# Expert weights in longer runs, one more slot for them, and embedding inputs on another DMA queue, in a hybrid transformer layer on one core

## The chip, the cores and the metric

The kernel runs on one core of a Trainium2 chip. The metric is the time of one execution on the device in microseconds (us), as the median of several runs. A core has five engines with instruction streams of their own: TensorE (PE; its weight loads, PEld, overlap its matmuls), VectorE (DVE), ScalarE (ACT), GpSimd (POOL) and SyncE (SP). SP computes nothing here; it issues DMAs. POOL issues DMAs too, the indirect ones (gather and scatter by row numbers) among them. All DMAs of the core are carried out by its 16 DMA engines.

## The reference

One layer over 1024 tokens of width 1024, in float32:

```
x = x + concat(attention(x), mlstm(x)) @ w_o          # norms, projections, two kinds of heads
h = rmsnorm(x) * g;  pick 1 of 4 groups, then 2 of its 8 experts for each token, weights w1, w2
y = (silu(h @ w_gate_e) * (h @ w_up_e)) @ w_down_e    # 32 experts, gate and up 1024 x 256, down 256 x 1024
x = x + w1 * y[first expert] + w2 * y[second expert]
x = x + (p @ w_ple) * sigmoid((rmsnorm(x) * g2) @ w_ple_gate)   # p: 1024 x 256, an embedding for each token
out = rmsnorm(x) * g3
```

## The kernel before

Matrix products keep float32 precision by splitting: each operand becomes `hi` (rounded to the short mantissa that TensorE reads as fp32r) and `lo` (the rest), and three matmuls stand for one (`mm3`, lines 127 to 129). A split (`split`, lines 132 and 133) is a copy to `hi` on ScalarE and a subtraction to `lo` on VectorE. Weights therefore arrive raw, are split, and only then multiplied.

The execution has four stages. Until about 430 us: projections, attention and mLSTM (the first stage). Until about 548: the output projection and the router, tile by tile of 128 tokens. Then the row numbers of each expert's tokens are worked out, and the expert stage runs from about 562 to 911. The last stage sums the experts' rows and does the embedding gate and the final norm.

*The expert stage* (`experts`). Each of the 32 experts takes a block of up to 128 tokens (rows beyond that go through a loop, `overflow`, which ran for no block here). For each expert: POOL gathers its tokens from `h2d` into `xg` (`moe_gather`, line 1149; two buffers, one gather is issued two experts ahead), TensorE transposes them (`xgp`, line 1159) and both halves are split to `xh`, `xl`; gate and up are one product of 512 columns (`gups`); `silu` and the product give `eh`, which is transposed (`ehp`, line 1179), split to `eht` and multiplied with the down weights (`eyps`); the rows go through `ey` by a scatter on POOL to `ybd` (line 1189).

*The weights of the experts.* An expert has three raw tiles of 128 partitions x 2048 floats, 1 MB each: two for gate and up (`rgu`, loaded by `load_gu`, each by one DMA for gate and one for up), one for down (`rdn`, `load_dn`). All go through the SP queue, but for the two `rgu` of expert 3, which POOL issues. `R()` hands out the slots for raw tiles from a ring (`rring`): four slots in the output stage (pool R1, tags R0 to R3), nine from the expert stage on (R4 to R8 in pool R2 are added). `W()` hands out nine slots (`NW`) for split weights in the same way; a raw tile fills two, an expert six. Loads are issued three experts ahead (`moe_load(e + 3)`); a load waits until the splits have freed its slot.

*The embedding.* Six of the eight tiles of `p @ w_ple` are computed between experts, behind experts 14, 16, 18, 20, 22 and 24 (`PLE_AT`): `ple_in(i)` (line 1285) loads 128 x 256 floats into `pin`, `ple_tile(i)` (line 1302) transposes them (`pps`, line 1305), splits them and multiplies. The load for a tile is written in the code one expert ahead of its use (`if e + 1 in PLE_AT[1:]`), the first one with `ple_load` at expert 5, and the last two in `final_load`. `pin` shares its four buffers with `eh` (tag "eh"), and its load goes through the SP queue. The results are kept in `ples`: each second tile takes one raw slot out of the ring for good (`retire`), three in all.

*What sets the order.* The code is written as a sequence with tiles and buffers; a scheduler orders each engine's instructions at build time, with `issue_after` and priorities as its limits. On the chip each engine, SP and POOL too, carries out its list strictly in that order: an issue that has to wait for a free buffer holds everything behind it on its queue.

Of the kernel before, what the change touches and what calls it, by code (L numbers as in the profile page):

```python
# [20 lines left out]
P = 128  # L21
T = 1024
D = 1024
# [4 lines left out]
DE = 256  # L28
# [31 lines left out]
class Kernel:  # L60
# [1047 lines left out]
        return w[e] if isinstance(e, int) else w[bass.ds(e, 1)].rearrange("o k f -> (o k) f")  # L1108

    def load_gu(self, e, b, q=None):  # L1110
        raw = self.R("rgu")
        v = raw.rearrange("p (k u f) -> p k u f", k=4, u=2)
        for u, n in enumerate(("w_gate_e", "w_up_e")):
            w = self.weight(n, e).rearrange("(p k) f -> p k f", k=KT)
            (q or self.nc.sync).dma_start(v[:, :, u, :], w[:, 4 * b:4 * b + 4, :])
        return raw

    def load_dn(self, e):
# [22 lines left out]
        return out  # L1141

    def split_gu(self, raws):
        return [(h[:, o:o + 512], l[:, o:o + 512]) for h, l in self.split_w(raws) for o in (0, 512)]

    def moe_gather(self, gcol):
        xg = self.xgs[self.ngather % len(self.xgs)]
# [135 lines left out]
        self.ple_in(0)  # L1283

    def ple_in(self, i):
        self.pin[i] = self.t("B", "pin", [P, DE], bufs=4, tag="eh")
        self.nc.sync.dma_start(self.pin[i], self.a["p"][0, 0, i * P:(i + 1) * P, :])

    def ple_half(self, k):
        raw = self.t("PL", "rple", [P, D])  # L1290
# [131 lines left out]
    def run(self):  # L1422
        self.raws, self.nr, self.nw = {}, 0, 0
        self.mixers()
        self.open("R1", "left")
        self.open("W1", "left")
        self.rring = [("R1", f"R{i}") for i in range(4)]
        self.wring = [("W1", f"W{i}") for i in range(6)]
        self.open("RT", "right")
        self.open("A3", "right")  # L1430
        self.open("psB", None, PSUM)
        self.out_weights()
        self.router_setup()
        gb = self.bcast("A3", self.a["norm_ffn_g"][0], "gb_ffn")
        end = None
        for i in range(NT):
            end = self.out_tile(i, gb, end)
            if i == 1:
                self.raws[0] = self.moe_load(0)
            if i == 4:  # L1440
                list(self.route_tiles(0, 4))
                self.first = self.split_gu(self.raws[0][:2]), self.split_w(self.raws[0][2:])
            if i == 5:
                self.raws[1] = self.moe_load(1)
        rt = self.route_tiles(4, 7)
        next(rt)
        end()
        list(rt)
        gu2 = self.load_gu(2, 0)
        self.close("A3")  # L1450
        list(self.route_tiles(7, 8))
        self.route_static()
        self.open("R2", "left")
        self.open("B", "left")
        self.rring, self.nr = [("R2", f"R{i}") for i in range(4, 9)] + [self.rring[(self.nr + i) % 4] for i in range(4)], 0
        more = [("B", f"W{i}") for i in range(6, 9)]
        self.wring += more[:NW - 6]
        self.rring[5:5] = more[NW - 6:]
        self.raws[2] = gu2, self.load_gu(2, 1), self.load_dn(2)
        self.moe_setup()  # L1460
        with self.tc.issue_after(self.stored.ins):
            gu3 = self.load_gu(3, 0, self.nc.gpsimd)
        with self.tc.issue_after(self.routed.ins):
            self.route_rest()
        self.experts(gu3)
        self.n_over = self.nc.values_load(self.nov[0:1, 0:1], min_val=0, max_val=15)
        self.final_load()
        self.overflow()
        self.final()
        self.finish()  # L1470
# [30 lines left out]
```

## Time and profile before

| | |
|---|---|
| time, median of 3 runs | 1031.0 us (1030.45 to 1031.9) |
| the profiled execution | 1031.45 us; span from the first to the last instruction 1029.7, so 1.75 around it |
| mean granted TensorE clock | 0.966 |
| busy: TensorE, VectorE, ScalarE, GpSimd | 953.9 us (93%), 805.8 (78%), 666.7 (65%), 165.7 (16%) |
| DMA queue of SP (q1) | 146.00 MB in 111502 packets, 42.4% of the 16 engines' span |
| software DMA queue (q0, issued by POOL) | 38.33 MB in 15776 packets, 10.4% |
| packets under 2 KB | 105070 of 127360 |

The busy share of an engine is a mean over all four stages, each of which has another limit. So the rows further down are of stretches of the execution: a window gives the busy time of each engine in it (with the count of its instructions), the granted clock of TensorE (1.00 is its upper level of 2.4 GHz, 0.50 the lower of 1.2) and the share and rate of the DMA engines. A timeline row is one instruction: its start, its duration, engine, line, and in brackets the idle time in front of it with what ended that. "SPq" marks time in which SP's queue was held on an instruction.

### The profile page before, as it was taken

Reading aid. Unit: us, or ns where it says so; the run is one execution under the profiler, and the core shown is the slowest. Engines: PE = TensorE matmul, PEld = TensorE weight load, DVE = VectorE, ACT = ScalarE, POOL = GpSimd, SP = SyncE. Lnnn points to the kernel's source line nnn. Section 1 sums busy time; section 2 is a strip of 40 time slices with the busy share of each in tenths; the row PEclk is TensorE's granted clock in tenths of the full one; section 3 lists DMA queues with packets and bytes.
Section 4 is the critical chain, followed back from the end, with each engine's and each line's share of the span. In section 5 each row is a group of like instructions: output and inputs, shape, how many; then the busy total and the mean of one; then the engine's idle time right before and its main releaser. Section 6 shows DMA issues by size and latency. Waiting matters only on the chain. (4 is left out here: it accounts for less than half of the span.)

```text
span 1029.7 us, 16040 instructions
## 1 busy us (share of the span) xinstructions
PE 953.9 (93%) x5583; PEld 819.2 (80%) x5583; DVE 805.8 (78%) x1877; ACT 666.7 (65%) x1182; POOL 165.7 (16%) x213
## 2 busy tenths in 40 slices
PE   4999999998999999899995989999699999979996
PEld 4999999996788888688884867888588888858875
DVE  7759788367888989774747899998678889858885
ACT  5554766254788889763333877998578788755432
POOL 4000000101222322101013121222112112210000
PEclk9999999999999999899996998999899999989999
DMA  7230111310000001698348898999999999774541
GB/s 220 101 101 25 42 62 59 102 37 11 17 11 14 13 12 23 229 295 288 123 159 272 261 359 283 354 351 343 338 301 315 341 304 356 243 254 173 184 164 61
DMA packets 127360, 185.36 MB, mean 180 GB/s; under 512 B 19487, under 2 KB 105070, under 8 KB 123182
## 3 DMA queue, kind: packets, MB, share of 16 engines
q1 hardware_dynamic: 111502, 146.00, 42.4%
q0 software_dynamic: 15776, 38.33, 10.4%
q8 instruction: 44, 0.72, 0.3%
q14 instruction: 38, 0.31, 0.1%
HBM read 167.48 MB, written 33.59 MB: 195 GB/s over the span
## 5 line engine op out<-in xcount | busy, mean ns | idle before, releaser
L133 DVE TENSOR_TENSOR w<-rgu,w 128x1024 fp32r<-128x1024 f32 x128 | 155.1, 1227 | 32.8 <-ACT w L132 29.6
L132 ACT ACTIVATE w<-rgu 128x1024 fp32r<-128x1024 f32 x128 | 133.3, 1065 | 6.1 <-PE gups L129 3.3
L127 PE MATMUL inp<-hh,win 128*128 128x256 f32 x384 | 111.7, 291 | 0.0
L129 PE MATMUL inp<-hh,win 128*128 128x256 f32 x384 | 111.1, 290 | 0.5 <-DVE win L256 0.5
L128 PE MATMUL inp<-hl,win 128*128 128x256 f32 x384 | 111.4, 291 | 0.1
L127 PE MATMUL gups<-w,xh 128*128 128x512 f32 x256 | 103.8, 405 | 0.0
L128 PE MATMUL gups<-w,xh 128*128 128x512 f32 x256 | 102.0, 398 | 0.0
L129 PE MATMUL gups<-w,xl 128*128 128x512 f32 x256 | 101.2, 395 | 0.0
L133 DVE TENSOR_TENSOR w<-rdn,w 128x1024 fp32r<-128x1024 f32 x64 | 77.2, 1219 | 2.7 <-ACT w L132 1.9
L129 PEld LDWEIGHTS inp<-hh,win 128*128 128x128 f32 x384 | 74.6, 195 | 0.7 <-DVE win L256 0.7
L128 PEld LDWEIGHTS inp<-hl,win 128*128 128x128 f32 x384 | 74.6, 194 | 0.5 <-DVE hl L133 0.4
L127 PEld LDWEIGHTS inp<-hh,win 128*128 128x128 f32 x384 | 74.5, 194 | 0.3 <-ACT z L331 0.2
L132 ACT ACTIVATE w<-rdn 128x1024 fp32r<-128x1024 f32 x64 | 66.0, 1067 | 4.1 <-PE gups L129 3.7
L1149 POOL DMA_INDIRECT xg<-h2d,gidx x32 | 37.1, 1159 | 179.2 <-PE xgp L1159 145.8
L1188 ACT ACTIVATE ey<-eyps 128x512 f32<-128x512 f32 x64 | 38.2, 596 | 40.4 <-PE eyps L129 30.8
L705 PE MATMUL po<-pt,V 128*128 128x256 f32 x320 | 61.2, 307 | 0.9 <-ACT pt L132 0.5
L133 DVE TENSOR_TENSOR pt<-ptp,pt 128x512 fp32r<-128x512 f32 (+2 forms) x112 | 54.3, 491 | 7.3 <-ACT pt L132 5.7
L132 ACT ACTIVATE pt<-ptp 128x512 fp32r<-128x512 f32 (+2 forms) x112 | 48.1, 443 | 14.7 <-PE ptp L693 7.4
L127 PE MATMUL eyps<-w,eht 128*128 128x512 f32 x128 | 54.5, 426 | 2.4 <-ACT eht L132 2.3
L129 PEld LDWEIGHTS gups<-w,xl 128*128 128x128 f32 x256 | 48.3, 189 | 9.5
L128 PEld LDWEIGHTS gups<-w,xh 128*128 128x128 f32 x256 | 48.6, 190 | 9.1
L127 PEld LDWEIGHTS gups<-w,xh 128*128 128x128 f32 x256 | 48.7, 190 | 9.0 <-ACT xh L132 0.2
(392 smaller groups left out, 2633.2 us busy)
## 6 DMA issues: line engine op xcount, KB each, us to landing
rdn<-in_w_down_e_dram SPq DMA_DIRECT2D x32, 1024.0 KB, 8.9
rgu<-in_w_gate_e_dram SPq DMA_DIRECT2D x62, 512.0 KB, 11.5
rgu<-in_w_up_e_dram SPq DMA_DIRECT2D x62, 512.0 KB, 10.0
wraw<-in_w_in_dram SPq DMA_DIRECT2D x11, 512.0 KB, 5.4
x<-in_x_dram SPq DMA_DIRECT2D x8, 512.0 KB, 4.6
abw<-mlrows SPq DMA_DIRECT2D x8, 512.0 KB, 3.7
mixf<-mixd SPq DMA_DIRECT2D x8, 512.0 KB, 5.7
xres<-in_x_dram SPq DMA_DIRECT2D x8, 512.0 KB
```

Of the source, the lines that this page charges most:

```text
L127: nc.tensor.matmul(out, w_hi, m_hi, start=start, stop=False)
L128: nc.tensor.matmul(out, w_hi, m_lo, start=False, stop=False)
L129: nc.tensor.matmul(out, w_lo, m_hi, start=False, stop=stop)
L132: a = self.nc.scalar.activation(hi, src, AF.Copy)
L133: v = self.nc.vector.tensor_sub(lo, src, hi)
L705: nc.tensor.matmul(po, self.V[kt][:, h, :], pts[t - 1][:, w, u, :], start=(kt + w == 0), stop=(kt == 2 * j + 1 and w == 1))
L1149: self.gathered = self.nc.gpsimd.indirect_dma_start(out=xg, out_offset=None, in_=self.h2d, in_offset=bass.IndirectOffsetOnAxis(ap=gcol, ax ...
L1188: nc.scalar.activation(y[:, s], py[c], AF.Copy)
```

## The change

Four edits.

1. A raw tile of gate and up held, in each partition, four runs of 512 floats, gate and up side by side, so that the DMA wrote and read 256 floats (1 KB) at a time. Now its first half holds gate and its second half up, 1024 floats in one run (4 KB). `split_gu` therefore no longer takes a flat run of 1024 for a split: it reads and writes through a view of 2 x 2 x 256 (half, row, column), and the split tiles are laid out as before.
2. The loads of `pin` are issued by POOL instead of SP, and `pin` has three buffers of its own instead of a share of the four of `eh`.
3. The scratch for DMA descriptors is set to 2048 bytes (16384 where nothing is said, an eighth), and a tenth raw slot (tag R9, pool R1) is in the ring, from the output stage on.
4. With the fifth slot of the output stage, the second half of expert 2's gate and up is loaded in front of `self.close("A3")`.

```
     def load_gu(self, e, b, q=None):
+
         raw = self.R("rgu")
-        v = raw.rearrange("p (k u f) -> p k u f", k=4, u=2)
         for u, n in enumerate(("w_gate_e", "w_up_e")):
             w = self.weight(n, e).rearrange("(p k) f -> p k f", k=KT)
-            (q or self.nc.sync).dma_start(v[:, :, u, :], w[:, 4 * b:4 * b + 4, :])
+            (q or self.nc.sync).dma_start(raw[:, u * D:(u + 1) * D].rearrange("p (k f) -> p k f", k=4),
+                                          w[:, 4 * b:4 * b + 4, :])
         return raw
...
     def split_gu(self, raws):
-        return [(h[:, o:o + 512], l[:, o:o + 512]) for h, l in self.split_w(raws) for o in (0, 512)]
+
+        out = []
+        side = lambda t: t.rearrange("p (k u f) -> p u k f", k=2, u=2)
+        for raw in raws:
+            v = raw.rearrange("p (u k f) -> p u k f", u=2, k=4)
+            for j in range(2):
+                hi, lo = self.W("w")
+                self.last_split = self.split(side(hi), side(lo), v[:, :, 2 * j:2 * j + 2, :])
+                out += [(hi[:, o:o + 512], lo[:, o:o + 512]) for o in (0, 512)]
+        return out
...
     def ple_in(self, i):
-        self.pin[i] = self.t("B", "pin", [P, DE], bufs=4, tag="eh")
-        self.nc.sync.dma_start(self.pin[i], self.a["p"][0, 0, i * P:(i + 1) * P, :])
+        self.pin[i] = self.t("B", "pin", [P, DE], bufs=3)
+        self.nc.gpsimd.dma_start(self.pin[i], self.a["p"][0, 0, i * P:(i + 1) * P, :])
...
-        self.rring = [("R1", f"R{i}") for i in range(4)]
+        self.rring = [("R1", f"R{i}") for i in (0, 1, 2, 3, 9)]
...
-        gu2 = self.load_gu(2, 0)
+        gu2 = self.load_gu(2, 0), self.load_gu(2, 1)
         self.close("A3")
...
-        self.rring, self.nr = [("R2", f"R{i}") for i in range(4, 9)] + [self.rring[(self.nr + i) % 4] for i in range(4)], 0
+        self.rring, self.nr = [("R2", f"R{i}") for i in range(4, 9)] + [self.rring[(self.nr + i) % 5] for i in range(5)], 0
...
-        self.raws[2] = gu2, self.load_gu(2, 1), self.load_dn(2)
+        self.raws[2] = *gu2, self.load_dn(2)
...
-    nc = bacc.Bacc("TRN2", target_bir_lowering=False, num_devices=1)
+    nc = bacc.Bacc("TRN2", target_bir_lowering=False, num_devices=1, dynamic_dma_scratch_size=2048)
```

On TensorE, VectorE and ScalarE the order of the instructions stays as it was but for a few neighbours that change places. On the two queues it moves. SP's list around the load of the second embedding input, before: `rgu` and `rdn` are raw expert weights, `pin` the embedding input.

```order
L1120 DMA rdn<-in_w_down_e_dram 128x2048
L1115 DMA rgu<-in_w_gate_e_dram 128x4x256
L1115 DMA rgu<-in_w_up_e_dram 128x4x256
L1287 DMA pin<-in_p_dram 128x256
L1115 DMA rgu<-in_w_gate_e_dram 128x4x256
L1115 DMA rgu<-in_w_up_e_dram 128x4x256
L1120 DMA rdn<-in_w_down_e_dram 128x2048
```

And in the changed kernel, at the same place:

```order
L1121 DMA rdn<-in_w_down_e_dram 128x2048
L1115 DMA rgu<-in_w_gate_e_dram 128x1024
L1115 DMA rgu<-in_w_up_e_dram 128x1024
L1121 DMA rdn<-in_w_down_e_dram 128x2048 x2
L1115 DMA rgu<-in_w_gate_e_dram 128x1024
L1115 DMA rgu<-in_w_up_e_dram 128x1024
```

The load of `pin` is gone from SP, and the weights stand without it; the pieces of gate and up are 1024 floats a partition instead of four times 256.

POOL's list from the first gathers of the expert stage to its first scatter, before; `xg` are the gathered tokens (two buffers, with a number behind the name), `ybd` the experts' results.

```order
L1149 DMA xg_6431<-h2d,gidx 128x1024
L1149 DMA xg_6432<-h2d,gidx 128x1024
L1115 DMA rgu<-in_w_gate_e_dram 128x4x256
L1115 DMA rgu<-in_w_up_e_dram 128x4x256
L1149 DMA xg_6431<-h2d,gidx 128x1024
L1149 DMA xg_6432<-h2d,gidx 128x1024
L1149 DMA xg_6431<-h2d,gidx 128x1024
L1149 DMA xg_6432<-h2d,gidx 128x1024
L1189 DMA ybd<-ey,sidx 2048x1024
```

The same stretch of POOL in the changed kernel:

```order
L1159 DMA xg_6431<-h2d,gidx 128x1024
L1159 DMA xg_6432<-h2d,gidx 128x1024
L1115 DMA rgu<-in_w_gate_e_dram 128x1024
L1115 DMA rgu<-in_w_up_e_dram 128x1024
L1159 DMA xg_6431<-h2d,gidx 128x1024
L1159 DMA xg_6432<-h2d,gidx 128x1024
L1297 DMA pin<-in_p_dram 128x256 x3
L1159 DMA xg_6431<-h2d,gidx 128x1024
L1159 DMA xg_6432<-h2d,gidx 128x1024
L1199 DMA ybd<-ey,sidx 2048x1024
```

Three loads of `pin`, as many as it has buffers, stand behind the fourth gather; the other five come later, each with a scatter to `ybd` ahead of it and one behind it.

## Rows read from the trace of the kernel before

**Rows 1.** Windows: us, busy (xcount) PE, PEld, DVE, ACT, POOL, clock, DMA share, GB/s.
```profile
640.00:680.00 40.00, 40.00 (x196) 33.12 (x195) 39.08 (x44) 36.77 (x54) 10.51 (x10) 1.00 1.00 353
720.00:760.00 40.00, 31.99 (x141) 25.85 (x140) 25.96 (x30) 25.06 (x38) 6.54 (x6) 0.87 0.92 317
800.00:840.00 40.00, 40.00 (x193) 32.73 (x192) 34.49 (x39) 33.40 (x50) 7.78 (x7) 1.00 0.94 315
```

**Rows 2.** Waits of TensorE, 400 to 1030 us: total us, count, mean us.
```profile
PE pps L1305 <- DMA pin<-in_p_dram: 7.5, 1, 7.5
PE xgp L1159 <- DMA xg<-h2d,gidx: 6.2, 1, 6.2
```

**Rows 3.** Timeline of TensorE: start and duration in us, idle time before in brackets.
```profile
711.81 0.39 PE L1179 MATMUL ehp<-ident,eh 128*128 128x128 f32 x2
712.04 0.40 PE L1305 MATMUL pps<-ident,pin 128*128 128x128 f32 x2
...
734.63 0.39 PE L1179 MATMUL ehp<-ident,eh 128*128 128x128 f32 x2
742.51 0.67 PE L1305 MATMUL pps<-ident,pin 128*128 128x128 f32 x2 [7.49 <-DMA pin<-in_p_dram]
742.84 0.77 PE L127 MATMUL gups<-w,xh 128*128 128x512 f32 x1
...
748.56 0.39 PE L127 MATMUL eyps<-w,eht 128*128 128x512 f32 x1
748.79 0.39 PE L128 MATMUL eyps<-w,eht 128*128 128x512 f32 x1
```

**Rows 4.** Timeline of the SP queue around the second embedding input.
```profile
722.04 2.18 SPq L1115 DMA_DIRECT2D rgu<-in_w_up_e_dram  x1
...
729.90 4.23 SPq L1287 DMA_DIRECT2D pin<-in_p_dram  x1
```

**Rows 5.** Timeline of POOL, 540 to 1030 us.
```profile
552.10 0.54 POOL L914 DMA_DIRECT2D x2d<-xres  x1
...
573.57 0.98 POOL L1149 DMA_INDIRECT xg<-h2d,gidx  x1 [4.86 <-PE xgp L1159]
...
719.02 1.36 POOL L1189 DMA_INDIRECT ybd<-ey,sidx  x1 [9.49 <-ACT ey L1188]
...
750.84 1.36 POOL L1189 DMA_INDIRECT ybd<-ey,sidx  x1 [18.71 <-ACT ey L1188]
...
772.89 1.35 POOL L1189 DMA_INDIRECT ybd<-ey,sidx  x1 [8.59 <-ACT ey L1188]
```

**Rows 6.** DMA issues, 640 to 720 us: count, KB each, median us to landing.
```profile
rgu<-in_w_gate_e_dram SPq DMA_DIRECT2D x14, 512.0 KB, 15.4
rgu<-in_w_up_e_dram SPq DMA_DIRECT2D x14, 512.0 KB, 12.1
...
xg<-h2d,gidx POOLq DMA_INDIRECT x8, 8.3
```

**Rows 7.** Window right behind the pause of TensorE.
```profile
742.00:748.00 6.00, 5.49 (x14) 4.44 (x15) 1.65 (x2) 1.33 (x2) 0.00 (x0) 0.50 0.96 356
```

**Rows 8.** Timeline of ScalarE: two splits of weights.
```profile
715.76 1.06 ACT L132 ACTIVATE w<-rgu 128x1024 fp32r<-128x1024 f32 x1 [2.81 <-DMA rgu<-in_w_up_e_dram]
...
743.50 1.05 ACT L132 ACTIVATE w<-rgu 128x1024 fp32r<-128x1024 f32 x1
```

**Rows 9.** Windows in which one kind of weight load ran alone.
```profile
542.00:544.00 2.00, 2.00 (x13) 1.65 (x11) 1.83 (x13) 0.60 (x1) 0.00 (x0) 1.00 0.88 207
546.00:550.00 4.00, 1.97 (x17) 1.59 (x16) 3.79 (x24) 1.38 (x4) 0.00 (x0) 1.00 1.01 417
```

**Rows 10.** Groups of VectorE by shape: busy us, mean ns, idle before, releaser.
```profile
L133 DVE TENSOR_TENSOR w<-rgu,w 128x1024 fp32r<-128x1024 f32 x128 | 155.1, 1227 | 32.8 <-ACT w L132 29.6 <-DMA rdn<-in_w_down_e_dram 0.5
...
L133 DVE TENSOR_TENSOR wq<-rawq,wq 128x768 fp32r<-128x768 f32 x2 | 1.9, 958 | 0.0
```

**Rows 11.** First line of the page.
```profile
span 1029.7 us, 16040 instructions
```

## The prediction

> **What bounds the kernel now.** I read the stretches first, then the waits of TensorE, then the pauses one by one on the engines and queues around them. In the expert stage the stretch 640 to 680 us has TensorE busy for all of its 40 us, VectorE for 39.08, and the DMA engines at share 1.00 with 353 GB/s; 800 to 840 again has TensorE at 40.00, with VectorE at 34.49 and DMA at 0.94 [rows 1]. So TensorE sets the pace there, and whatever another engine or a queue saves is worth nothing unless TensorE stands still for it. Between them lies one stretch that differs: 720 to 760, TensorE busy 31.99 of 40 and granted clock 0.87 [rows 1].
>
> The waits of TensorE after 400 us name the reason: the longest is the transpose `pps` of an embedding tile, 7.5 us, once, for the DMA of `pin` [rows 2]. The reader is to see in its timeline that the transposes `ehp` start at 734.63 and `pps` only at 742.51, while for the embedding tile before, `ehp` at 711.81 is followed by `pps` at 712.04 [rows 3]. The SP queue tells why the input is late: the load of that `pin` stands behind a run of expert weights, SP reaches it at 729.90, and is held on it for 4.23 us [rows 4]. ScalarE and VectorE stand still with TensorE, because their next instruction in order is the split of `pps`.
>
> **The change, part by part.**
>
> *Embedding inputs on the GpSimd queue, in three buffers of their own.* The order of the change has three `pin` loads on POOL right behind the fourth gather and ahead of the fifth. In the trace of before the fifth starts at 573.57 after 4.86 us of idle time [rows 5]. An issue on POOL costs about 0.54 us (the nearest row, a plain store of 128 rows [rows 5]), three 1.6 us, all inside that idle time. So the input of the second embedding tile is issued near 570 and used near 735; even the slowest median landing in the row list, 15.4 us [rows 6], leaves it 150 us early. The wait goes.
>
> What it is worth: `pps` follows `ehp` by 712.04 - 711.81 = 0.23 us when its input is there [rows 3], so it moves from 742.51 to 734.63 + 0.23 = 734.86: 7.65 us. Behind the pause the clock is at 0.50, its lower level of 1.2 GHz, from 742 to 748 [rows 7]: fourteen matmuls of 512 columns start from 742.84 up to 748.56, in 5.72 us, where the next two starts are 0.23 us apart [rows 3], so 14 x 0.23 = 3.22 would do: 2.50 us. Without the pause TensorE has been running for over 100 us before, as in 640 to 680 where the clock was 1.00. Together 10.15 us. A check by another view: the scatter of the expert in front of an embedding tile starts at 719.02, 750.84 and 772.89 [rows 5]; a pair of experts with one embedding tile takes 772.89 - 750.84 = 22.05 when undisturbed and 31.82 here: 9.77 us. I take 10.0.
>
> What is late next: the weight split on ScalarE that follows `pps`. It started at 743.50 [rows 8] and now could at 743.50 - 7.65 = 735.85. The second half of its tile was issued at 722.04 [rows 4]; with the median 12.1 us to landing of that queue [rows 6] it is there at 734.1, in time. Later loads are asked for at 315 GB/s (800 to 840), under the 353 that the engines gave at share 1.00 [rows 1], so the lateness does not grow. Value zero; upper end in the first rival.
>
> The five later loads add a wait on POOL: a buffer is free when the transposes of the tile three before are done. Behind the fourth load on POOL stand a scatter and two gathers. The first tile's `pps` is at 712.04 [rows 3], that scatter at 719.02 [rows 5]: 7 us to spare. For the fifth load it is 734.86 against 750.84 less 10. Nothing.
>
> The Trainium skill speaks against this part (DMA: Bandwidth & Descriptors, Issuing engines are not separate DMA queues): DMAs of all queues run on the same 16 engines and interleave, so another issuing queue saves issue time only. By that rule the queue alone is worth little; here it is the early place on it that counts. What the rule alone would leave is the second rival.
>
> *4 KB runs for gate and up.* A pure stretch of the old pattern (gate and up of one tile in 1 KB pieces, 542 to 544) moved 207 GB/s at share 0.88; one of the down weights in 8 KB pieces (546 to 550) 417 GB/s at share 1.01 [rows 9]. So a piece four times as long is moved faster, by something between nothing and a factor 417 x 0.88 / (207 x 1.01) = 1.76 in engine time. The end does not see it: TensorE is at 40.00 of 40 in the saturated stretch as well [rows 1]. What it buys is cover: ScalarE's wait of 2.81 us for a weight at 715.76 [rows 8] should go, and the loads after 735 arrive sooner. If that cover were missing, see the first rival. Value zero, between 0 and 2.8 us saved.
>
> The Trainium skill has a rule by which this part does nothing (DMA: Bandwidth & Descriptors, Specifications: full rate from 512 B on, so 1 KB already has it). The two stretches above disagree, and the measurement decides; by either the sum is the same.
>
> *The splits read two halves of a tile in a walk of 2 x 2 x 256.* VectorE and ScalarE lose their flat access of 1024. No row has three levels; the nearest has two: 768 elements of `rawq` in eight pieces took 958 ns against 1227 for 1024 flat ones [rows 10]. At the same cost for each element, a split without its fixed part would be 1227 x 0.75 = 920, so strided access costs at most 38 ns, and less if there is a fixed part. Value zero, between -0.02 and 0.04 us for a split; the price if it is more is the last rival.
>
> *Tenth slot, descriptor scratch cut to an eighth.* Before the expert stage one more half tile is loaded early, and in it the loads run one slot ahead; no wait of TensorE there is for weights [rows 2], so this is worth zero now. A short ring has no row. It costs nothing at the least. At the most, a gather may have to stand until the one DMA before it has landed, 8.3 us by the landing of gathers [rows 6]; on the path that is only the first, for which TensorE waits 6.2 us already [rows 2]; in turn, weights that come earlier or faster beside it could shorten that wait, by all of the 6.2 at most. I take zero for both: by the code POOL's issues carry few pieces, each a row of 2 to 4 KB, and the largest store (512 B pieces) is in the first stage, with POOL far ahead.
>
> *The sum.* The profiled execution took 1031.45 us (span 1029.7 [rows 11] and 1.75 around it); less 10.0 it is 1021.45. The median of the runs shown is 1031.0, 0.45 below; the forecast for the median is 1021.2.
>
> **The rivals.**
>
> 1. *Weights take the place of the input.* For it: DMA at 1.00 and a wait for a weight at 715.76 [rows 1, 8]. If longer pieces gain nothing and the load of 722.04 takes the longer 15.4 us [rows 6], it lands at 737.4, 1.6 us after 735.85; if TensorE then stops, the slow clock comes back for 2.5 us. 1021.2 + 4.1 = 1025.3. Against it: by the code nine slots hold split weights, where an expert takes six, so the splits run ahead of TensorE; and the loads before 735 were faster. 8%.
>
> 2. *The input comes at the old time.* If POOL in fact reaches the load only next to its use, at about 729.90 as SP did, the same 16 engines serve it as they serve a gather: 8.3 us [rows 6], 738.2. The pause is then 738.2 - 734.86 = 3.3 us, the slow clock stays; 4.3 of the 10 us are gained: 1026.7. Against it: the order. 5%.
>
> 3. *The change does not take away what holds `pps`.* The profile infers the releaser and gives no landing for this load. Against it: 8.4 us from the end of its issue (734.13) to 742.51 fit a landing in that queue. No difference: 1031. 4%.
>
> 4. *Slower: the split walks cost VectorE.* Place: 640 to 680 and what is like it, about 625 to 735. VectorE has 0.92 us free in these 40, with 44 instructions, at ten for an expert (six weight splits, four others) 4.4 experts: 9.1 us and 0.21 us free for each, twelve experts in 110 us [rows 1]. Four splits for each expert change; at p us more each, the stage grows by 12 x (4p - 0.21). It decides from p = 0.26 us, where the 10 us are eaten; at 0.3 it is 11.9, 1033.1. After 735 VectorE has 5.5 us free in 40 (800 to 840 [rows 1]), enough. Against it: the 38 ns above. 5%.
>
> **How the numbers follow.** Forecast 78%, rivals 8, 5, 4 and 5%. Within 0.2% (what a measurement can tell from no change, 2.1 us) lies the third alone: 4%. Slower 5%, faster 91%. The forecast's own range is 1017 to 1023.5: the two ways to reach the sum differ by 0.4 us, a saved 2.8 us and part of the first gather's wait go down, walks and ring go up. With the first and the better part of the second rival the range is 1017 to 1026.5.
>
> **What would show it.** Right: no wait of `pps` for `pin` near 735, and TensorE busy with clock 1.00 from about 625 to 900; the three `pin` issues on POOL near 570; splits of gate and up at 1.21 to 1.27 us on VectorE; fewer packets under 2 KB and less DMA share at the same pace; gathers issued right after their transposes. Wrong: a wait of ScalarE for `rgu` near 736 that TensorE shares, gaps before gathers on POOL that end with a DMA, or VectorE's splits above 1.4 us.

## The result and the profile after

The changed kernel takes 1022.35 us (1020.31 to 1023.98, 4 runs), against 1031.05 for the kernel before (4 runs): ratio 0.9916, 95% interval [0.9901, 0.9931], 8.7 us less. A second measurement beside other kernels gave 0.9913 [0.9885, 0.9942], 1024.04 us. The forecast was 1021.2. The profiled execution is the quickest of its four, 1020.31 us with a span of 1018.5.

Windows of the changed kernel (us, busy with counts of TensorE, weight loads, VectorE, ScalarE, GpSimd; then clock, DMA share, GB/s); the first, second and last answer to [rows 1], the third to [rows 7].

```profile
640.00:680.00 40.00, 40.00 (x196) 33.07 (x195) 38.84 (x45) 36.75 (x54) 11.10 (x10) 1.00 0.98 361
720.00:760.00 40.00, 40.00 (x191) 32.73 (x190) 33.57 (x39) 32.53 (x48) 9.51 (x9) 1.00 0.97 354
...
742.00:748.00 6.00, 6.00 (x31) 4.83 (x30) 5.65 (x8) 5.07 (x7) 0.61 (x1) 1.00 1.01 379
...
800.00:840.00 40.00, 40.00 (x194) 32.73 (x194) 32.79 (x40) 32.83 (x51) 9.26 (x8) 1.00 0.93 329
```

The reader is to see that 720 to 760 is now like its neighbours: TensorE 40.00 of 40 instead of 31.99, clock 1.00 instead of 0.87, and between 742 and 748 31 matmuls instead of 14. The timeline of TensorE at the second embedding tile, which answers to [rows 3]:

```profile
733.22 0.39 PE L1189 MATMUL ehp<-ident,eh 128*128 128x128 f32 x2
733.44 0.40 PE L1315 MATMUL pps<-ident,pin 128*128 128x128 f32 x2
```

`pps` follows `ehp` by 0.22 us, without a wait. The whole pause with its slow clock is read from the next transpose `ehp`, first before and then after:

```profile
757.28 0.39 PE L1179 MATMUL ehp<-ident,eh 128*128 128x128 f32 x2
```
```profile
745.76 0.39 PE L1189 MATMUL ehp<-ident,eh 128*128 128x128 f32 x2
```

From `ehp` to `ehp` it was 757.28 - 734.63 = 22.65 us and is 745.76 - 733.22 = 12.54: 10.11 us less. TensorE's waits after 400 us (total, count, longest) no longer have the first line of [rows 2]:

```profile
PE xgp L1169 <- DMA xg<-h2d,gidx: 6.8, 2, 5.9
PE cnt L970 <- DVE M L967: 5.7, 1, 5.7
```

POOL's timeline shows the three early loads (it answers to the gather at 573.57 of [rows 5]), and SP's that an issue of weights takes 0.33 us where it took 2.18 [rows 4] (the issues of gate and up between 640 and 745 us take 0.33 to 0.44 us, where they took 0.37 to 5.96):

```profile
566.70 1.00 POOL L1159 DMA_INDIRECT xg<-h2d,gidx  x1 [1.73 <-PE xgp L1169]
567.69 1.72 POOL L1297 DMA_DIRECT2D pin<-in_p_dram  x3
572.61 1.05 POOL L1159 DMA_INDIRECT xg<-h2d,gidx  x1 [3.21 <-PE xgp L1169]
```
```profile
720.59 0.33 SPq L1115 DMA_DIRECT2D rgu<-in_w_gate_e_dram  x1
722.41 0.33 SPq L1115 DMA_DIRECT2D rgu<-in_w_up_e_dram  x1
```

The splits on VectorE cost what they did, 1227 ns in the 2 x 2 x 256 view against 1227 flat [rows 10]; the packets fell by almost four in ten, from 127360 to 78976, at the same bytes:

```profile
L133 DVE TENSOR_TENSOR w<-rgu,w 128x1024 fp32r<-128x1024 f32 x128 | 155.0, 1227 | 29.0 <-ACT w L132 24.6 <-DMA rgu<-in_w_up_e_dram 0.7 <-DMA rgu<-in_w_gate_e_dram 0.7
...
DMA packets 78976, 185.36 MB, mean 182 GB/s; under 512 B 19487, under 2 KB 40558, under 8 KB 74798
```

So far everything stands as forecast. What the forecast had not seen came out when the parts were taken one by one.

### The profile page after: what moved, and what is told of

Same layout as the page of the kernel before. It is cut to its first block, busy times and chain, and to the rows that moved or that the text cites. A ratio compares the mean times of both kernels' runs of the same rounds, so it can differ in the third digit from the quotient of the medians.

```text
span 1018.5 us, 16023 instructions
## 1 busy us (share of the span) xinstructions
PE 946.1 (93%) x5583; PEld 812.3 (80%) x5583; DVE 805.9 (79%) x1877; ACT 666.9 (65%) x1182; POOL 174.0 (17%) x221
## 2 busy tenths in 40 slices
DMA packets 78976, 185.36 MB, mean 182 GB/s; under 512 B 19487, under 2 KB 40558, under 8 KB 74798
## 5 line engine op out<-in xcount | busy, mean ns | idle before, releaser
L133 DVE TENSOR_TENSOR w<-rgu,w 128x1024 fp32r<-128x1024 f32 x128 | 155.0, 1227 | 29.0 <-ACT w L132 24.6
L1159 POOL DMA_INDIRECT xg<-h2d,gidx x32 | 39.8, 1244 | 178.1 <-PE xgp L1169 135.3
L128 PEld LDWEIGHTS gups<-w,xh 128*128 128x128 f32 x256 | 48.3, 189 | 9.2
L127 PE MATMUL wops<-wo,mixh 128*128 128x512 f32 x128 | 52.5, 412 | 3.4 <-ACT wo L132 3.4
```

The source lines that it names most:

```text
L127: nc.tensor.matmul(out, w_hi, m_hi, start=start, stop=False)
L128: nc.tensor.matmul(out, w_hi, m_lo, start=False, stop=False)
L133: v = self.nc.vector.tensor_sub(lo, src, hi)
L1159: self.gathered = self.nc.gpsimd.indirect_dma_start(out=xg, out_offset=None, in_=self.h2d, in_offset=bass.IndirectOffsetOnAxis(ap=gcol, ax ...
```

## The experiments

Ratios are to the kernel before, run beside on the same chip; "loss" and "gain" are against it.

**One part of the embedding loads, or all of it.** Three kernels change only the loads of `pin`: queue and buffers, buffers only, queue only. The first two need 3 KB of room a partition (three buffers of 256 floats), which the short scratch gives.

```
pin_pool_own     pin: bufs=3, nc.gpsimd.dma_start;  dynamic_dma_scratch_size=2048
pin_sp_own       pin: bufs=3, nc.sync.dma_start;    dynamic_dma_scratch_size=2048
pin_pool_shared  pin: bufs=4, tag="eh", nc.gpsimd.dma_start
```

> The kernel before with the embedding inputs alone moved: issued by POOL, three buffers of their own (short descriptor scratch, without which the buffers find no room; nine slots, 1 KB runs). Theory P (the early place of the load is all): three loads near 568 us on POOL, no wait of pps for pin, TensorE busy 40 of 40 us from 640 to 880, 1021 to 1023 us, as the whole change. Rival R (the longer runs carry part of it: at 1 KB the weights are late as soon as the pause no longer lets them catch up): a wait for rgu behind 735, 1024 to 1028 us.

> The same, but the loads stay on SP; with three buffers of their own the first three stand early in SP's list, the others some experts ahead of their use. Theory P: the queue plays no part, 1021 to 1023 us, no wait for pin. Rival Q (a small load on SP stands behind weights wherever it is put, and only POOL's queue is quick): a later input is late or the loads hold up weights, 1026 to 1031 us.

> The kernel before with the loads of pin on POOL and nothing else: they share the four buffers of eh, so the second one stands late, between two gathers. Theory P with POOL free of a backlog: the load is issued by about 720 and lands 8 us later, before 735; no pause, but the gather behind it waits with it for the buffer: 1021 to 1024 us. The second rival of the prediction (at a late place the queue gives only half): pause of about 3 us, 1025 to 1028 us. If the buffer is what is late (a product eh three experts back must be transposed first), the pause stays: 1030 us.

Measured: 1.0037 [1.0022, 1.0052], 1.0022 [1.0013, 1.0032] and 0.9984 [0.9968, 1.0000]. Theory P missed: the pause at 735 is gone in all three (in the third a wait for `pin` of 2.8 us is left, at 905), yet two are slower than before, and the third gains about 2 us, with an interval that reaches 1. The first of TensorE's waits in `pin_pool_own` tells half of it:

```profile
PE wops L127 <- ACT mixh L132: 9.0, 1, 9.0
PE xgp L1159 <- DMA xg<-h2d,gidx: 6.1, 1, 6.1
```

A wait of 9.0 us that the kernel before does not have, in the output stage at about 440 us, where no embedding is touched. `pin_sp_own` has the same line. `pin_pool_shared`, with the full scratch, does not have it. In that kernel POOL reaches the second load only at 724.57, some 13 us ahead of its use at 737.45, and it is in time:

```profile
723.30 1.27 POOL L1149 DMA_INDIRECT xg<-h2d,gidx  x1 [0.30 <-PE gups L129]
724.57 0.62 POOL L1287 DMA_DIRECT2D pin<-in_p_dram  x1
732.41 1.04 POOL L1149 DMA_INDIRECT xg<-h2d,gidx  x1 [7.22 <-PE xgp L1159]
```

So 12 us from the end of its issue to its use were enough; it was issued 5.3 us before SP reached it in the kernel before [rows 4], since no weights stood ahead of it on POOL. So either is enough against the pause at 735: another queue at a late place (here 5.3 us earlier than SP was, and used 2.6 us later than before), or an early place on the same queue.

**The longer runs alone.**

```
load_gu, split_gu as in the change; all else as before
```

> The kernel before with the 4 KB runs alone (gate and up in two halves, splits in the strided view). Theory P: worth nothing by itself, the load of pin stands at its old place on SP and the pause stays: 1029 to 1032 us. Rival H (in the changed kernel SP's issues of weights take 0.33 us in the stretch where they took 0.4 to 4.8 before: it is the 1 KB pieces that hold SP, and with them gone SP reaches the load of pin in time): wait for pin under 2 us, 1021 to 1024 us. The splits on VectorE 1.20 to 1.27 us in both.

Measured: 0.9997 [0.9981, 1.0013]. The rival is refuted, and in an instructive way (SP's queue, then TensorE):

```profile
730.25 0.38 SPq L1297 DMA_DIRECT2D pin<-in_p_dram  x1
...
737.70 0.39 PE L1189 MATMUL ehp<-ident,eh 128*128 128x128 f32 x2
745.21 0.67 PE L1315 MATMUL pps<-ident,pin 128*128 128x128 f32 x2 [7.12 <-DMA pin<-in_p_dram]
```

SP is no longer held on the load: 0.38 us instead of 4.23 [rows 4]. But the input comes 745.21 - 730.63 = 14.6 us after the issue, where it took 8.4 before. Where these went can be counted, since the 128 rows of `pin` (1 KB) are now the only packets between 512 B and 2 KB. DMA packets of this kernel from 733 to 735, 735 to 737, 741 to 743 and 743 to 745.5 us:

```profile
DMA packets 254, 0.78 MB, mean 389 GB/s; under 512 B 27, under 2 KB 91, under 8 KB 243
DMA packets 217, 0.53 MB, mean 264 GB/s; under 512 B 78, under 2 KB 110, under 8 KB 203
...
DMA packets 172, 0.70 MB, mean 352 GB/s; under 512 B 26, under 2 KB 34, under 8 KB 140
DMA packets 248, 0.91 MB, mean 362 GB/s; under 512 B 28, under 2 KB 44, under 8 KB 235
```

"Under 2 KB" less "under 512 B" is 64, 32, 8 and 16: three quarters of the load are through by 737, eight rows follow up to 741, and the last 24 come after that. I read the lateness as time in line behind the weights issued ahead of it, on a part of the engines, and SP's being held as the share of it that shows in SP's timeline when the pieces are short. That is not shown: the packets were not told apart by engine.

**Where the 9 us in the output stage come from.** The scratch alone, and the loads of `pin` with just as much room as they need:

```
scratch      dynamic_dma_scratch_size=2048
pin_own_13k  pin: bufs=3, nc.gpsimd.dma_start;  dynamic_dma_scratch_size=13312
```

> The kernel before with the short descriptor scratch alone. Theory S (the room that it leaves free moves SP's list in the output stage, and TensorE waits some 9 us for mixh there): 1036 to 1041 us, with the pause for pin as before. Rival (the short ring itself holds POOL's gathers or stores): gaps in front of gathers that end with a DMA, and a loss spread over the expert stage. Prediction: the scratch is worth nothing, 1030 to 1032.

> As the first of these runs (embedding inputs on POOL with three buffers of their own, nothing else), but with a descriptor scratch of 13312 instead of 2048: just the room the buffers need, so that SP's list in the output stage stays that of the kernel before. Theory S (the first run lost 9 us to a wait for mixh in the output stage, which came with the room that the short scratch left free, not with the loads): that wait is gone. Theory W (without the pause the 1 KB weights are late): TensorE lacks some 4 us of 80 between 720 and 800, 1024 to 1027 us. Theory P (the early load is all): 1020.5 to 1022.5. If 1031 or more: neither, the loads on POOL themselves cost the time.

Measured: 1.0071 [1.0046, 1.0096] (7.3 us lost, as theory S has it) and 0.9965 [0.9948, 0.9982] (3.6 us gained, 1027.35 us, the wait for `mixh` gone; nearest to theory W). ScalarE in `scratch`, and in the kernel before:

```profile
433.05 7.67 ACT L132 ACTIVATE wo<-rawo 128x1024 fp32r<-128x1024 f32 x8
440.62 1.04 ACT L132 ACTIVATE mixh<-mixf 128x1024 fp32r<-128x1024 f32 x1
```
```profile
431.54 1.04 ACT L132 ACTIVATE mixh<-mixf 128x1024 fp32r<-128x1024 f32 x1
432.49 3.89 ACT L132 ACTIVATE wo<-rawo 128x1024 fp32r<-128x1024 f32 x4
```

With 14 KB free in each partition (16384 less 2048 bytes) the scheduler puts the four loads of the raw output weights (`rawo`) seven rows earlier in SP's list, in front of the router's weights. SP reaches them some 208 us earlier (`scratch`, then the kernel before):

```profile
216.29 31.28 SPq L818 DMA_DIRECT2D rawo<-in_w_o_dram  x4
```
```profile
424.43 7.22 SPq L818 DMA_DIRECT2D rawo<-in_w_o_dram  x4
```

All eight of their splits then stand in front of the split of the first tokens, `mixh`, on ScalarE. TensorE's first matmul of this stage needs `mixh`; its wait is the 9.0 us above, 7.67 of them for these splits. That free room is the cause is read from the runs side by side: the three kernels that leave 11 or 14 KB free have the wait, and none of the others, which leave 6 KB or less (the tenth slot takes 8). POOL's gathers in `scratch` show no wait on a DMA: the short ring itself costs nothing that can be seen. In the change the tenth slot takes up most of the room, and `mixh` is split at 431.49, ahead of `wo`, as before.

**What eats the rest of the 10 us.** In `pin_own_13k` SP's list in the output stage is the old one and the pause is gone, yet 3.6 us are gained and not 10. ScalarE's timeline between 736 and 800:

```profile
742.12 1.06 ACT L132 ACTIVATE w<-rgu 128x1024 fp32r<-128x1024 f32 x1 [1.99 <-DMA rgu<-in_w_up_e_dram]
...
754.43 2.01 ACT L132 ACTIVATE w<-rgu 128x1024 fp32r<-128x1024 f32 x2 [0.84 <-DMA rgu<-in_w_up_e_dram]
...
767.76 1.06 ACT L132 ACTIVATE w<-rgu 128x1024 fp32r<-128x1024 f32 x1 [3.13 <-DMA rgu<-in_w_up_e_dram]
```

And TensorE's windows there:

```profile
720.00:760.00 40.00, 37.92 (x179) 30.28 (x178) 32.02 (x37) 31.94 (x49) 8.80 (x9) 1.00 0.98 335
760.00:800.00 40.00, 38.19 (x174) 30.25 (x173) 29.81 (x37) 28.55 (x44) 9.32 (x7) 0.96 0.98 338
```

The weights are late, as the first rival of the prediction had it. From 600 to 912 us ScalarE waits 9.0 us for `rgu` in five places, where the kernel before waits 2.8 in one. Between the transposes `ehp` at 746.40 and 784.20 lie 37.8 us; in the changed kernel the same stretch takes 777.39 - 745.76 = 31.6, as it does in the kernel before behind its pause:

```profile
746.40 0.39 PE L1179 MATMUL ehp<-ident,eh 128*128 128x128 f32 x2
...
784.20 0.39 PE L1179 MATMUL ehp<-ident,eh 128*128 128x128 f32 x2
```
```profile
777.39 0.39 PE L1189 MATMUL ehp<-ident,eh 128*128 128x128 f32 x2
```

The 6.2 us between are what the late weights cost, and 10.1 - 6.2 = 3.9 fits the 3.6 gained. In the kernel before no split behind the pause waits for `rgu`, so the pause had been giving the DMA engines 10 us to catch up. The same weights were late in `pin_pool_shared`: 9.4 us of ScalarE's waits between 700 and 800.

**Which part covers it.** The longer runs or the slot added to the moved loads, one without the other:

```
pin_own_4k_13k  as pin_own_13k, with load_gu and split_gu of the change (nine slots)
pin_slot        the change with load_gu and split_gu of before (ten slots, 1 KB)
```

> The same with the 4 KB runs of gate and up, scratch 13312, nine slots. Theory W: TensorE 40 of 40 us in 720 to 800, and with it the whole gain of the change, 1020 to 1023 us. Rival T (it is the tenth slot that lets the weights run ahead): 1024 to 1027 us as without the runs. Theory P: 1021 to 1023, the same as without them.

> The changed kernel with the old 1 KB runs (embedding inputs on POOL, tenth slot, short scratch). With nine slots and 1 KB runs ScalarE waited 9.0 us for rgu between 636 and 800. Theory U (both cover late weights; each alone leaves some): ScalarE's wait for rgu 2 to 6 us there, 1023 to 1026 us. Theory T (the slot alone is enough, the runs are worth nothing): wait under 1 us, 1021 to 1023. Theory V (the runs decide, the slot only takes up room): 1026 to 1029.

Measured: 0.9976 [0.9961, 0.9992] and 0.9980 [0.9959, 1.0000]. Neither alone gains more than the moved loads by themselves (0.9965), and the two together gain 5 us more. Longer runs with nine slots shorten ScalarE's wait for `rgu` between 636 and 800 from 9.0 to 3.0 us, but a wait for the raw embedding weights appears, and TensorE follows it at 641 with a wait of 2.9 (from the sixth transpose `ehp` to the seventh it takes 14.1 us there, 10.3 in `runs_4k` and 9.6 in the kernel before):

```profile
ACT w L132 <- DMA rgu<-in_w_up_e_dram: 3.0, 2, 2.1
ACT wp L132 <- DMA rple<-in_w_ple_dram: 2.9, 1, 2.9
```

Ten slots with 1 KB leave the stretch from 746 to 778 whole (747.92 to 779.53, 31.6 us) and are late further on, the largest time before the split at 789.67:

```profile
789.67 1.06 ACT L132 ACTIVATE w<-rgu 128x1024 fp32r<-128x1024 f32 x1 [3.85 <-DMA rgu<-in_w_up_e_dram]
```

There ScalarE's wait for `rgu` is 12.1 us from 600 to 912, against 1.1 in the changed kernel. The late weights are not gone but elsewhere: from `ehp` to `ehp`, `pin_slot` is 1.6 us longer than the changed kernel just before 735, 3.4 between 780 and 805 and 2.7 between 868 and 890, together more than the 7.1 by which `pin_own_13k` is longer up to 784. Theory U holds in its direction (both are needed), not in its size: 2 to 6 us of wait were expected between 636 and 800, and it was 7.8. The time of `pin_slot`, 1028.58, is the one that theory V gives, but by V the longer runs with nine slots should have gained, and they did not. Why one slot more only moves the lateness at 1 KB stays open, and so does how the slot and the longer runs together cover it.

**The change without its largest part, and the slot alone.**

```
no_pin  the change with pin as before (SP, tag "eh")
slot10  before, with the tenth slot, the short scratch, the earlier half tile
```

> The changed kernel with the embedding inputs as before (SP, sharing the buffers of eh): longer runs, tenth slot, short scratch. If the load of pin is what the whole gain hangs on: a wait of pps for pin of 3 to 8 us and 1028 to 1032 us. If the slot moves SP's list enough to bring it in time: no wait, 1021 to 1023 us.

> The kernel before with the tenth slot, the short scratch and the earlier half tile of expert 2 alone. By the prediction worth nothing: 1029 to 1032 us, pause of pps for pin as before. Rival: one slot more moves SP ahead of its backlog, so that the load of pin is reached in time: 1021 to 1024 us. Theory S: with the room of the scratch taken by the slot, no wait of 9 us for mixh in the output stage.

Measured: 1.0029 [1.0013, 1.0046] and 1.0064 [1.0034, 1.0094]: both slower than before. In `slot10` the pause has grown from 7.5 to 11.1 us; in `no_pin` it is 6.3:

```profile
PE pps L1305 <- DMA pin<-in_p_dram: 11.1, 1, 11.1
```
```profile
PE pps L1315 <- DMA pin<-in_p_dram: 6.3, 1, 6.3
```

With one slot more, two more loads of weights stand in front of the input on the same queue: SP issues its load at 736.56 in `slot10` instead of reaching it at 729.90 [rows 4]. With 4 KB runs they do no harm: `no_pin` issues it at 730.67, `runs_4k` with nine slots at 730.25, and the pause is 6.3 against 7.1 us. So the pause is not the whole loss. The rest lies in a stretch near the end of the expert stage. From the 28th transpose `ehp` to the 30th it takes 18.96 to 19.03 us in each of the eight kernels with nine slots, and 19.4 and 20.4 in the two executions of the change, 21.9 in `no_pin`, 22.1 in `pin_slot`, 22.2 in `after_sp` and 23.2 in `slot10`. ScalarE waits for weights there (`slot10`, then `no_pin`):

```profile
881.86 1.06 ACT L132 ACTIVATE w<-rgu 128x1024 fp32r<-128x1024 f32 x1 [3.64 <-DMA rgu<-in_w_up_e_dram]
```
```profile
879.66 1.06 ACT L132 ACTIVATE w<-rgu 128x1024 fp32r<-128x1024 f32 x1 [3.05 <-DMA rgu<-in_w_up_e_dram]
```

So the tenth slot with its earlier half tile brings late weights of its own, in the changed kernel too; why it does so there stays open. In `slot10` the longer pause (3.5 us) and this stretch (4.2) cover the loss; in `no_pin` this stretch is 2.9 us longer and the pause 1.1 shorter, and 3.3 us lie ahead of the first expert, where two executions of the change also differ by 3.4.

**The early place on SP, and the change once more.**

```
after_sp     the change with nc.sync.dma_start for pin (three own buffers)
after_again  the change
```

> The changed kernel with the embedding inputs on SP again, but in their three own buffers: the first three stand at place 82 of SP's list. If only the early place counts: as the changed kernel, 1021 to 1023 us. If POOL's queue is needed in the full change: a later input holds weights, or is late: 1024 to 1030.

> The changed kernel once more, beside the others on the same chip, for the size of its gain: 1021 to 1023.5 us, ratio 0.990 to 0.993.

Measured: 0.9945 [0.9924, 0.9965], 1026.19 us; and 0.9913 [0.9885, 0.9942], 1024.04 us. The intervals overlap, so whether POOL's queue is worth the 2 us between them is open. No wait for `pin` is left in either, and from the seventh transpose `ehp` to the 28th, with the six embedding tiles between experts, their profiled executions take 218.0 us each: the queue makes no difference there.

## Why the prediction was right, and where its working was wrong

*The pause (10.0 us).* Right in place, mechanism and size: 10.11 us from transpose to transpose, the sum of 7.65 and 2.50 was 10.15. The clock stays at 1.00 behind it, and the three loads are issued at 567.69 (said: near 570) inside POOL's idle time.

*What is late next (value zero).* In the full change right: the split that follows `pps` starts at 734.22 without a wait, and ScalarE waits 0.2 us for `rgu` from 636 to 800. But the reason given was wrong. The argument that later loads are asked for at 315 GB/s, under 353, "so the lateness does not grow", set the need of a later stretch against a rate at its best. The changed kernel, with nothing late, moves 366 and 354 GB/s between 680 and 760. With the loads moved and all else as before, the engines ran at 335 to 338 GB/s with share 0.98, and the weights fell behind by 6.2 us of TensorE's time. The first rival had this mechanism, at 1025.3 us; the kernel in which it happened, `pin_own_13k`, took 1027.35. In the change it did not come true because the other two parts cover it; the reasons given against it, that the splits run ahead and the earlier loads were faster, did not keep it from happening in `pin_own_13k`.

*4 KB runs (zero, and cover).* Zero alone (0.9997), as said, and cover beside the moved loads, but only together with the slot (0.9976 without it). How much the longer pieces give in a mixed stretch can now be put in: from 680 to 720 us 344 GB/s at share 0.99 before, 366 at 0.98 after:

```profile
680.00:720.00 40.00, 40.00 (x195) 32.95 (x194) 35.47 (x41) 33.90 (x49) 9.86 (x8) 1.00 0.99 344
```
```profile
680.00:720.00 40.00, 40.00 (x195) 33.08 (x194) 36.79 (x42) 35.10 (x52) 12.10 (x10) 1.00 0.98 366
```

For the same share that is (366 / 0.98) / (344 / 0.99) = 1.07, near the lower end of the 1 to 1.76 that the pure stretches gave [rows 9]. The rule of the Trainium skill (DMA: Bandwidth & Descriptors, Specifications: full rate from 512 B) is off by these 7% here; a mean over everything in flight comes closer to it than the pure stretches do. The other rule of the Trainium skill (same page, Issuing engines are not separate DMA queues: another queue saves issue time only) is in keeping with the runs: POOL issued the load 5.3 us before SP got to it, and SP was held 4.23 us more, which is more than the pause; that the engines then served POOL's load any sooner is not shown (at most 12 us, against 8.4 and 14.6 behind SP).

*Slot and scratch (zero).* This step failed. That no wait of TensorE is for weights, "so this is worth zero now", held for the kernel before, with the pause in it. Once that is gone, the slot and the longer runs together are worth about 5 us (0.9965 without both, 0.9916 with both), and the slot alone (with the short scratch and the earlier half tile) costs 6.6. And the scratch was looked at only as a ring of descriptors; its cost lies in the room it leaves, which moved a scheduler's order some 290 us ahead of the pause and was worth 7.3 us. The sum came out right because the slot fills that room again, and because slot and runs give back the 6 us that the moved loads alone lose to late weights. That these two zeros cancel was not foreseen: so far the nearness of the forecast is luck.

*The rivals.* The second is refuted by its condition: POOL issues the load at 567.69, not near 729.90. (In `pin_pool_shared` an issue at 724.57 left no pause; what one at 729.90 on POOL would leave was not tested.) The third is refuted by the trace: `pps` no longer waits. The fourth is refuted by 1227 ns.

*The range.* The profiled run is 11.1 us below that of the kernel before, the medians 8.7. Of the 11.1, 10.1 are the pause; another 0.8 were gained from the `ehp` ahead of it (the forecast put the cover of the longer runs at 0 to 2.8) and 1.6 up to the sixth `ehp`, and 1.3 were lost between the sixth and the seventh and near the end of the expert stage. In a second profiled execution of the changed kernel (span 1024.4) ScalarE waits again for `rgu`, 3.2 us in two places, and 1.6 for `rple`:

```profile
ACT w L132 <- DMA rgu<-in_w_up_e_dram: 3.2, 2, 1.9
```

These waits make its expert stage 1.8 us longer in two places, but 3.4 of the 5.9 us between the two executions lie ahead of the first expert (its `ehp` starts at 577.66 and 581.02). So late weights are a part of what lies between the forecast and the medians (1.2 and 2.8 us); what makes the rest, and why one execution has them and the next not, was not settled.

## What to carry to other kernels

A pause on the busiest engine is also the time in which its supply catches up: before counting it as a gain, compare what the transfers are asked for without it with what they moved while late, not with their best. A small load in a queue of large ones can come late (8.4 and 14.6 us behind its issue here), and a deeper prefetch puts more in front of it: with 1 KB pieces that cost 3.5 us more, with 4 KB pieces nothing. An early place or another queue both cured it. A slot added for prefetch can itself cost time elsewhere: look at its last uses. Freed memory is an edit of its own where a scheduler decides the order: look at the order far from the change.

## What was not expected of the hardware

With 1 KB pieces SP was held 2.18 us on an issue of weights and 4.23 on a small one [rows 4]; with 4 KB pieces an issue took 0.33 to 0.44 us between 640 and 745 us at DMA share 0.97 to 0.98, and the small load took 14.6 us from its issue to its use instead of 8.4. The rows of one load of 128 KB came 8 to 12 us apart. A descriptor scratch of an eighth showed no wait of POOL's gathers and scatters, of 128 rows each, on a DMA.
